# A 4-byte GpSimd mark tile made 128 bytes wide, in an encoder layer on one Trainium2 core: every later on-chip buffer starts 96 bytes higher

## The chip, the cores and the metric

The kernel runs on one NeuronCore of one Trainium2 chip. The metric is the device time of one execution, in microseconds, as the median of several executions. Before the change it is 2389.97 us, the median of 3 (2389.43 to 2391.98). The execution that was profiled took 2390.31 us, and the span from its first to its last instruction is 2388.5 us.

## What is computed

One encoder layer is applied to two inputs of 1024 rows by 1024 channels with the same weights. Cut to what matters:

```python
xn = rmsnorm(x, g_pre)
fv, fg, hv, hg, mg = split(xn @ w_in)                     # 8192 columns
fz  = fftn(fv as (L, 4 groups, 256), axes=(L, 256)).real   # Fourier branch
y_f = (fz * silu(fg)) @ w_fourier_out
v, x1, x2 = split(short_conv(hv, w_short))                # width 3
z = v
for n, gate in enumerate((x1, x2)):                       # Hyena branch
    z = gate * long_conv(z, filters[n], hyena_d[n])       # by FFT of 2L
y_h = (z * silu(hg)) @ w_hyena_out
g_f, g_h = split(sigmoid(mg + b_merge))
out = (g_f * y_f + g_h * y_h) @ w_out
return x + rmsnorm(out, g_post)
```

All data is float32. The filters are made inside the kernel, too.

## The kernel before, in words

A product of two float32 matrices is made of three TensorE products: both factors are split into a rounded high part and a low rest (`split`: ScalarE rounds, VectorE or GpSimd subtracts), and high by high, high by low and low by high are added in PSUM (`mm3`, `times`, and `mm`, whose line 193 issues nearly every product). Every product first loads its stationary factor (128 by 128 floats, 512 bytes in each partition) and then streams its moving factor past it: 512 columns (2048 bytes in each partition) in the large products, 256 to 260 in the transforms.

Four stages follow each other. In the profiled execution they lie about so: the Fourier branch of both inputs (`phase_fourier`, 0 to 200 us); the filters' spectra, with the input projections of the first input between them (`phase_main`, 200 to 680 us); the Hyena branch of both inputs (`branches`, 680 to 1690 us); the remaining gates, the output nets and the last projection (`phase_tail`, from 1690 us).

- `inproj` (from line 838) makes one block of 128 channels of the input projection. Its stationary factors are `wh` and `wl`, in pool `wp`; its moving factors are the 16 tiles `x0..` and `x1..` in pool `xp`, which hold the normalized input. Its sums are called `pin`.
- `forward` and `conv_back` make the transforms of the convolutions: `pX` (tables `cfwd` against `bh`, `bl`) and `pT` (`yh`, `yl` against tables `cinv`), 256 columns each.
- In `phase_tail` the gates (sums `pg`) take some stationary factors from `wp` (`wh`, `wl`, `w`) and some from pool `gw` (`s1h` to `s4l`, `a2h`, `a2l`, `wa`), against moving tiles in `xp` (`x..`, `oB..`) or pool `gs` (`room..`). The nets (sums `pn`) take all of them from `gw` and `xp`, under the names `wh` and `wl` as well.

The change touches `branches` (lines 1100 to 1103). There, `self.due` is a list of 30 transfers that build sums of the output weights in DRAM. They are issued by GpSimd, one in each step of the Hyena branch while the list lasts. Each is held back until a GpSimd copy of one column of the step's result `z` into the tile `mark` has been made, so that it isn't issued earlier. `mark` is the last tile that is asked for from pool `wp`.

Buffers are placed by pool, in the order in which pools are opened, each tile at a multiple of 32 bytes in every partition. `wp` is opened first after the Fourier stage (`open_x`), then `xp`, then the pools of `phase_main` and, in their place, those of `phase_tail`. So the size of `wp` sets where all of these begin. The tiles of the Fourier stage lie in the same space earlier, from pools of their own that begin where `wp` does.

Of the kernel before, what the change touches and what calls it, by code (L numbers as in the profile page):

```python
# [10 lines left out]
F32R = mybir.dt.float32r  # L11
# [5 lines left out]
P = 128  # L17
# [143 lines left out]
class K:  # L161
# [878 lines left out]
    def branches(self, nb, nct, ws):  # L1040

        tc, nc = self.tc, self.nc
        steps = []
        for b in range(nb):
            steps.append((b, 0, 0))
            for c in range(1, nct):
                steps += [(b, 0, c), (b, 1, c - 1)]
            steps.append((b, 1, nct - 1))  # L1050
        plain = list(self.PLAIN)
        Z, X, G = {}, {}, {}

        def front(i):
            b, n, c = steps[i]
            src = self.conv(1, c, ws, "v", b) if n == 0 else Z.pop(c)
            return self.conv_front(src, ws)

        def gates(i):
            b, n, c = steps[i]  # L1060
            x = self.conv(2 + n, c, ws, f"x{n + 1}", b)
            if n and b == 0:
                early = c < NH
                ps = None if early else self.inproj(4, c)
                sg = [self.wp.tile([P, 512], F32, tag="gt", name="sg", bufs=3) for q in range(2)]
                for q in range(2):
                    s = slice(512 * q, 512 * q + 512)
                    if early:
                        nc.sync.dma_start(sg[q], self.d_g[0][4][c][:, s])
                    else:  # L1070
                        nc.scalar.activation(sg[q], ps[:, s], AF.Silu)
                G[i] = sg, early
            X[i] = x

        def close(i):

            if i in G:
                sg, early = G.pop(i)
                for q in range(2):
                    s = slice(512 * q, 512 * q + 512)  # L1080
                    if early:
                        with tc.issue_after(self.rounded.ins):
                            nc.scalar.activation(sg[q], sg[q], AF.Silu)
                    self.mul("dve", X[i][:, s], X[i][:, s], sg[q])
        B = front(0)
        gates(0)
        for i, (b, n, c) in enumerate(steps):
            nxt = None
            if i + 1 < len(steps):
                nxt = front(i + 1)  # L1090
                gates(i + 1)
                if i + 2 < len(steps) and steps[i + 2][0] != steps[i + 1][0]:
                    self.load_x(steps[i + 2][0])
            y = self.conv_back(n, c, B, ws)
            close(i + 1)
            B = nxt
            for _ in range({4: 1, 3: 1, 2: 2, 1: 2}.get(len(steps) - i, 0)):
                self.spill_gate(b, *plain.pop(), ws)
            z = self.gate(n, c, y, X.pop(i))
            if self.due:  # L1100
                mark = self.wp.tile([P, 1], F32R, tag="mark", name="mark", bufs=1)
                with tc.issue_after(nc.gpsimd.tensor_copy(mark, z[:, 0:1]).ins):  # L1102
                    self.due.pop(0)()
            if n == 0:
                Z[c] = z
                continue
            nc.sync.dma_start(self.d_sh[b][c], z)
            if b == 0 and NF <= c:
                self.spill_gate(0, 0, c, ws)
        with tc.issue_after(self.ended.ins):  # L1110
            for sec, c in plain:
                self.spill_gate(1, sec, c, ws)
# [601 lines left out]
```

## Time and profile before

| What | Before |
|---|---|
| median of 3 executions | 2389.97 us |
| profiled execution, its span | 2390.31 us, 2388.5 us |
| TensorE busy | 2341.1 us, 98% of the span, 12784 products |
| VectorE busy | 1971.1 us, 83% |
| ScalarE busy | 1110.1 us, 46% |
| GpSimd busy | 452.9 us, 19% |
| DMA, mean rate | 201 GB/s |
| TensorE clock granted | 0.996 of full speed |

How to read it: products are pipelined. The duration of one in the profile runs from its start to the end of its results, while the next one starts long before. What a product costs a saturated TensorE is the distance from its start to the next one's start, which a stretch of the chain of waits or of the timeline gives when it is divided by the number of products in it. A row of the profile that groups instructions names the line, the engine, the operation, what is written and what is read (moving factor first, stationary factor second), the shapes and the count.

### The profile page before, as it was taken

To read this page: it belongs to the slowest core of one execution; us is meant where nothing else is said; L and a number is where in the kernel's file an instruction comes from. 1 tells how busy PE (TensorE), PEld (TensorE's weight loads), DVE (VectorE), ACT (ScalarE), POOL (GpSimd) and SP (SyncE) were. 2 spreads that over 40 slices of the span, in tenths; PEclk is the share of its full clock that TensorE was granted. 3 is DMA by queue.
4 is the path that set the end of the run, shared out by engine and by line. 5 is a ranking of instruction groups with operands and counts; after the bars stand their busy time and mean duration, and the time that the engine had idled before them with its cause. 6 is when DMAs were issued, how large, how long until landed. Compare 5 with 4: busy or idle time off the path is not lost.

```text
span 2388.5 us, 36189 instructions
## 1 busy us (share of the span) xinstructions
PE 2341.1 (98%) x12784; PEld 2013.8 (84%) x12784; DVE 1971.1 (83%) x3430; ACT 1110.1 (46%) x2072; POOL 452.9 (19%) x428
## 2 busy tenths in 40 slices
PE   6999999999989999999999999999999999999998
PEld 5998888888878888888888888888888888888787
DVE  7775789888788999999888999997655578787987
ACT  6654557767653433334223232333443464556443
POOL 3342231222323333232000000112000000101311
PEclk9999999999999999999999999999999999999999
DMA  7636895555556567667464565455554678998654
GB/s 260 213 135 216 291 322 177 166 170 166 191 184 209 188 213 208 209 196 251 153 201 143 172 189 162 147 159 166 201 164 138 222 257 271 269 311 247 195 160 141
DMA packets 246208, 479.71 MB, mean 201 GB/s; under 512 B 24582, under 2 KB 82280, under 8 KB 245706
## 3 DMA queue, kind: packets, MB, share of 16 engines
q1 hardware_dynamic: 222013, 402.25, 51.8%
q0 software_dynamic: 23792, 75.11, 11.1%
q8 instruction: 101, 1.65, 0.3%
q14 instruction: 81, 0.66, 0.1%
q10 hardware_dynamic: 221, 0.04, 0.0%
HBM read 326.82 MB, written 177.73 MB: 211 GB/s over the span
## 4 chain that ended last, share of the span: by engine, by line
PE 49%; issue 5%; DVE 4%; DMA 3%; POOL 0%; ACT 0%; DVEq 0%; SPq 0%; POOLq 0%; ACTq 0%
PE pin L193 19%; PE pg L193 14%; PE pn L193 5%; PE pT L193 5%; PE pX L193 5%; DMA d_m<-gt 1%; PE tph L904 1%; DVE x L176 0%; DMA oB<-d_wo 0%; DMA g<-d_g 0%; DMA k<-d_k 0%; DVE wl L180 0%; DVE t L180 0%; POOL d_m L1359 0%; DVE gt L180 0%
## 5 line engine op out<-in xcount | busy, mean ns | idle before, releaser
L193 PE MATMUL pin<-x,wh 128*128 128x512 f32 x2816 | 901.9, 396 | 7.5 <-DVE x L176 7.5
L193 PEld LDWEIGHTS pin<-x,wh 128*128 128x128 f32 x2816 | 523.5, 188 | 119.7 <-issue 7.6
L193 PE MATMUL pin<-x,wl 128*128 128x512 f32 x1408 | 558.1, 397 | 0.0
L180 POOL TENSOR_TENSOR wl<-wr,wh 128x512 fp32r<-128x512 f32 x128 | 229.8, 1796 | 670.6 <-ACT wh L170 621.1
L193 PEld LDWEIGHTS pin<-x,wl 128*128 128x128 f32 x1408 | 265.0, 188 | 55.1
L193 PE MATMUL pn<-room,wh 128*128 128x512 f32 x864 | 266.5, 389 | 0.2 <-DVE room L180 0.2
L193 PEld LDWEIGHTS pn<-room,wh 128*128 128x128 f32 x864 | 162.1, 188 | 34.3 <-DVE room L180 0.6
L193 PE MATMUL pn<-room,wl 128*128 128x512 f32 x432 | 168.4, 390 | 0.6 <-DVE wl L180 0.5
L180 DVE TENSOR_TENSOR t<-pX,k 128x1024 f32<-128x1024 f32 x128 | 155.4, 1214 | 10.1 <-PE pX L193 6.8
L193 PE MATMUL pX<-bh,cfwd 128*128 128x256 f32 x768 | 162.2, 288 | 0.0
L193 PE MATMUL pT<-cinv,yh 128*128 128x256 f32 x768 | 145.6, 284 | 1.4 <-DVE T0s L180 1.4
L170 ACT CAST wh<-wr 128x512 fp32r<-128x512 f32 x128 | 79.1, 618 | 142.6 <-PE pin L193 106.2
L170 ACT CAST bh<-b 128x512 fp32r<-128x512 f32 x144 | 88.4, 620 | 113.2 <-DVE b L180 78.8
L193 PEld LDWEIGHTS pT<-cinv,yh 128*128 128x128 f32 x768 | 122.9, 190 | 8.6 <-ACT T1s L957 1.5
L193 PEld LDWEIGHTS pX<-bh,cfwd 128*128 128x128 f32 x768 | 127.1, 190 | 2.6
L1359 POOL DMA_DIRECT2D d_m<-gt x32 | 27.2, 849 | 536.4 <-DVE gt L180 498.1
L170 ACT CAST yh<-y 128x512 fp32r<-128x512 f32 x96 | 59.6, 621 | 126.9 <-DVE y L180 126.4
L180 DVE TENSOR_TENSOR bl<-b,bh 128x512 fp32r<-128x512 f32 x144 | 107.1, 748 | 7.8 <-ACT bh L170 7.7
L193 PE MATMUL pT<-cinv,yl 128*128 128x256 f32 x384 | 109.0, 284 | 0.0
L193 PE MATMUL pX<-bl,cfwd 128*128 128x256 f32 x384 | 109.0, 284 | 0.0
L1102 POOL CAST mark<-x 128x1 fp32r<-128x1 f32 x30 | 21.6, 720 | 411.2 <-DVE x L176 411.0
L180 DVE TENSOR_TENSOR y<-t 128x512 f32<-128x512 f32 x128 | 91.7, 717 | 7.3 <-PE pT L193 6.9
(359 smaller groups left out, 5154.4 us busy)
## 6 DMA issues: line engine op xcount, KB each, us to landing
k<-d_k SPq DMA_DIRECT2D x128, 512.0 KB, 4.2
wr<-in_w_in SPq DMA_DIRECT2D x128, 256.0 KB, 3.4
d_g<-gt SPq DMA_DIRECT2D x124, 256.0 KB, 2.8
wl<-d_s SPq DMA_DIRECT2D x56, 512.0 KB, 5.5
d_k<-kt SPq DMA_DIRECT2D x128, 128.0 KB, 2.3
d_k<-kt SPq DMA_DIRECT2D x64, 256.0 KB, 2.8
g<-d_g SPq DMA_DIRECT2D x64, 256.0 KB, 5.2
r<-d_g SPq DMA_DIRECT2D x60, 256.0 KB, 5.8
```

The costliest lines, as they stand in the source:

```text
L170: self.rounded = nc.scalar.copy(h, src)
L180: return e.tensor_tensor(out, a, b, op=op)
L193: return self.nc.tensor.matmul(out, lhsT, rhs, start=start, stop=stop, skip_group_check=shared)
L904: nc.tensor.transpose(tp[:, q * P:(q + 1) * P], eo[:, e, q], self.ident)
L1102: with tc.issue_after(nc.gpsimd.tensor_copy(mark, z[:, 0:1]).ins):
L1359: nc.gpsimd.dma_start(dst, t, accum_op=ADD)
```

## The change

```diff
             z = self.gate(n, c, y, X.pop(i))
             if self.due:
-                mark = self.wp.tile([P, 1], F32R, tag="mark", name="mark", bufs=1)
-                with tc.issue_after(nc.gpsimd.tensor_copy(mark, z[:, 0:1]).ins):
+                mark = self.wp.tile([P, 32], F32R, tag="mark", name="mark", bufs=1)
+                with tc.issue_after(nc.gpsimd.tensor_copy(mark[:, 0:1], z[:, 0:1]).ins):
                     self.due.pop(0)()
```

The copy still writes one column. On all five engines the same instructions stand in the same order with the same waits as before; only addresses differ. The 4 bytes took a place of 32, and the 128 bytes take a place of 128, so everything behind the tile starts 96 bytes higher. This is where the built programs put some of the tiles (byte in each partition, and what is left when it is divided by 128 and by 512):

```
tile                            before              after
                                byte   /128 /512    byte   /128 /512
wp: wh, first of 3 buffers      17760   96  352     17760   96  352
wp: wr, w, first of 2           30048   96  352     30048   96  352
wp: mark                        40288   96  352     40288   96  352
xp: x00, moving of inproj       40320    0  384     40416   96  480
xp: x10                         44416    0  384     44512   96  480
cfwd / bh                  107904/184192 0  384  108000/184288  96 480
gs: room0                      105856    0  384    105952   96  480
gw: s2h                        181632    0  384    181728   96  480
gw: s4h                        193920    0  384    194016   96  480
nets' wh, in xp                 73088    0  384     73184   96  480
```

Further tiles of a kind follow at multiples of 2048 or 4096 bytes, and the four stationary blocks within a tile at multiples of 512. So before, in the products `pin`, the stationary factor starts 32 bytes short of where the moving factor does, counted modulo 512, and after it 128 bytes short; so it is with those of the `pg` whose stationary factor is in `wp`. In the other `pg` and in `pn`, `pX` and `pT` both factors start at the same place modulo 512, before and after. Tiles that begin before `mark`, and the whole Fourier stage, keep their addresses.

## The prediction

> **What bounds the kernel now.** I read the busy shares first, then the chain of waits, then the groups of products.
>
> ```profile
> PE 2341.1 (98%) x12784; PEld 2013.8 (84%) x12784; DVE 1971.1 (83%) x3430; ACT 1110.1 (46%) x2072; POOL 452.9 (19%) x428
> ...
> L193 PE MATMUL pin<-x,wh 128*128 128x512 f32 x2816 | 901.9, 396 | 7.5 <-DVE x L176 7.5
> ...
> L193 PE MATMUL pin<-x,wl 128*128 128x512 f32 x1408 | 558.1, 397 | 0.0
> ...
> L193 PE MATMUL pn<-room,wh 128*128 128x512 f32 x864 | 266.5, 389 | 0.2 <-DVE room L180 0.2
> ...
> L193 PE MATMUL pn<-room,wl 128*128 128x512 f32 x432 | 168.4, 390 | 0.6 <-DVE wl L180 0.5
> ```
>
> TensorE is busy for 98% of the span, and the largest groups of products wait 7.5 us in all before them. The time is the number of products times the distance between their starts. The reader should look at the mean durations here: products of one shape, 128x512, take 396 or 397 ns as `pin` and 389 or 390 ns as `pn`. The chain of waits, which gives stretches with nothing but products, has the same difference in the distances:
>
> ```profile
> 1659.04 27.76 PE pin L193 x119
> ...
> 1933.88 114.10 PE pn L193 x502
> ```
>
> 27.76 us / 119 = 233.3 ns for a `pin`, 114.10 us / 502 = 227.3 ns for a `pn`. Is it the stage or the operands? The groups of `pg`, which all lie in one stage, answer that (minimum, median and maximum duration, then first and last start):
>
> ```profile
> L193 PE MATMUL pg<-x,wh x176: 393/395/397, 1700.3 to 1897.4; 128*128 128x512 f32 x176
> L193 PE MATMUL pg<-room,s2h x160: 387/389/398, 1692.1 to 2368.5; 128*128 128x512 f32 x160
> ...
> L193 PE MATMUL pg<-oB,wh x120: 393/395/397, 2226.1 to 2360.4; 128*128 128x512 f32 x120
> L193 PE MATMUL pg<-x,s4h x96: 389/389/389, 1705.8 to 1919.2; 128*128 128x512 f32 x96
> L193 PE MATMUL pg<-x,wl x88: 389/394/397, 1700.7 to 1897.6; 128*128 128x512 f32 x88
> ...
> L193 PE MATMUL pg<-oB,s4h x64: 389/389/389, 2243.9 to 2379.4; 128*128 128x512 f32 x64
> L193 PE MATMUL pg<-oB,wl x60: 389/394/499, 2227.4 to 2360.6; 128*128 128x512 f32 x60
> ...
> L193 PE MATMUL pg<-x,wa x24: 389/389/389, 1686.6 to 1691.9; 128*128 128x512 f32 x24
> L193 PE MATMUL pg<-oB,w x12: 393/395/397, 2223.3 to 2225.9; 128*128 128x512 f32 x12
> ```
>
> The same moving tiles `x` and `oB` give 389 ns against `s4h` or `wa` and 394 or 395 ns against `wh`, `wl` or `w`. So it hangs on the stationary factor, and the longer products are exactly those with one from pool `wp`, whose tiles start at 96 modulo 128 bytes where all others start at 0. The timeline of TensorE gives the price: starts 2.10 us apart, then 2.04 us apart, with nine products between them in each case.
>
> ```profile
> 1700.25 0.63 PE L193 MATMUL pg<-x,wh 128*128 128x512 f32 x2
> ...
> 1702.35 0.63 PE L193 MATMUL pg<-x,wh 128*128 128x512 f32 x2
> ```
>
> ```profile
> 1705.84 0.61 PE L193 MATMUL pg<-x,s4h 128*128 128x512 f32 x2
> ...
> 1707.88 0.61 PE L193 MATMUL pg<-x,s4h 128*128 128x512 f32 x2
> ```
>
> 2.10 / 9 = 233.3 ns and 2.04 / 9 = 226.7 ns: a step of 6.6 ns in a product.
>
> **The change part by part.** No instruction is added, removed or moved. The copy into the mark writes the same 128x1, lies on GpSimd and costs what it did. What changes is where the buffers behind it start: 96 bytes higher, although the words of the change say a multiple of 128, since 4 bytes already took 32.
>
> The engines beside TensorE and the transfers first. Before the change some of their operands lie at 96 modulo 128 and others at 0, so the nearest rows bound what the shift costs them:
>
> ```profile
> L170 ACT CAST bh<-b 128x512 fp32r<-128x512 f32 x144 | 88.4, 620 | 113.2 <-DVE b L180 78.8 <-PE pX L193 24.6 <-PE pXf L193 9.0
> ...
> L170 ACT CAST wh<-wr 128x512 fp32r<-128x512 f32 x128 | 79.1, 618 | 142.6 <-PE pin L193 106.2 <-issue 25.1 <-DMA wr<-in_w_in 7.0
> ...
> L180 DVE TENSOR_TENSOR yc<-q 128x512 f32<-128x512 f32 x64 | 41.7, 691 | 0.0
> ...
> L180 DVE TENSOR_TENSOR gt<-gt,g 128x512 f32<-128x512 f32 x48 | 33.2, 691 | 2.0
> ```
>
> ```profile
> wh<-d_w SPq DMA_DIRECT2D x48, 256.0 KB, 3.2
> ...
> x<-d_x SPq DMA_DIRECT2D x32, 256.0 KB, 5.7
> ```
>
> `wh`, `wr` and `gt` lie at 96, `bh`, `b`, `yc` and `q` at 0: ScalarE 618 against 620 ns, VectorE 691 against 691 ns. A load of 256 KB lands after 3.2 us at 96 and after 5.7 us at 0 (in bursts, so this shows only that 96 is not the slow place). I take nothing for all of these, between a gain of 2 ns and a loss of 2 ns in each of the 3430 and 2072 instructions of VectorE and ScalarE, which TensorE covers but for the stretch below.
>
> Now TensorE. Products that take 233.3 ns now: 2816 + 1408 `pin` and, in `pg`, 176 + 88 + 120 + 60 + 12 = 456, in all 4680. After the change their moving factor lies at 96 modulo 128, like their stationary factor, which stays. In the 226.7 ns products both factors lie at 0, and after the change both lie at 96. If what counts is that both start alike modulo 128, then the 4680 come down to the lower distance and the others keep it. I price that with the smaller step, from the chain, 233.3 - 227.3 = 6.0 ns: 4680 x 6.0 ns = 28.1 us. By the timeline's step it is 4680 x 6.6 ns = 30.9 us.
>
> Does all of it reach the end? What is late next is VectorE, where it has no idle time left (busy time and count of PE, PEld, DVE, ACT and POOL in stretches of 100 us; below it PE's for `pin` alone):
>
> ```profile
> 800.00:900.00 100.00, 100.00 (x590) 87.72 (x589) 98.06 (x155) 36.16 (x66) 41.90 (x44) 1.00 0.67 206
> 900.00:1000.00 100.00, 98.65 (x595) 86.95 (x594) 96.44 (x150) 33.41 (x60) 29.43 (x36) 1.00 0.68 210
> 1000.00:1100.00 100.00, 100.00 (x592) 87.72 (x591) 100.00 (x163) 37.46 (x70) 36.88 (x36) 1.00 0.68 196
> 1100.00:1200.00 100.00, 100.00 (x562) 86.36 (x561) 90.27 (x147) 33.64 (x61) 4.24 (x7) 1.00 0.61 207
> ```
>
> ```profile
> 1000.00:1100.00 100.00, 66.94 (x268) 48.08 (x266) 12.70 (x10) 6.65 (x7) 1.00 0.68 196
> ```
>
> In the stretch from 1000 us VectorE is busy for 100.00 of 100 us, so the 268 x 6.0 ns = 1.6 us that TensorE would save there are lost. The two stretches before it have 1.9 and 3.6 us of VectorE left, which is just enough; if VectorE can't use them, three times 1.6 = 4.8 us are lost. The sum: 2390.3 (the profiled execution) - 28.1 + 1.6 = 2363.8 us, so **2364 us**. The median of the runs, 2389.97, lies 0.3 us below the profiled one, which I leave out.
>
> The Trainium skill says the contrary of the premise: the page "TensorE: Matmul & The Clock Gate", in Part 2 under "Step-by-step: what each phase is for", gives TensorE two independent read ports, so that loading the next weights takes no read bandwidth from the running product. Its page "SBUF — State Buffer" counts in lines of 16 bytes (its section on the DMA port swizzle, in the note on cachelines). By these two 96 bytes are six whole lines, nothing meets, and the sum is 2390. The rows above don't agree with that: 395 against 389 ns for the same moving tile.
>
> **The rivals.**
>
> *It stays as it is.* What counts could be a longer period than 128. Modulo 512 the pairs of the 4680 start 32 bytes apart now and 128 bytes apart after the change; only equal starts are seen with 226.7 ns. For this speaks a pair of transforms with 256 columns. In the Fourier stage the factors `eh` and `wo` start 128 apart modulo 512, those of `pT` start alike:
>
> ```profile
> 150.06 0.28 PE L193 MATMUL pfv<-wo,el 128*128 128x256 f32 x1
> ...
> 151.48 0.28 PE L193 MATMUL pfv<-wo,el 128*128 128x256 f32 x1
> ```
>
> ```profile
> 1630.15 0.28 PE L193 MATMUL pT<-cinv,yl 128*128 128x256 f32 x1
> ...
> 1630.87 0.28 PE L193 MATMUL pT<-cinv,yl 128*128 128x256 f32 x1
> ```
>
> 1.42 us / 12 products = 118.3 ns, 0.72 us / 6 = 120.0 ns. So 128 apart isn't the same state as 0 apart. Against it: that state is 1.7 ns shorter there, not longer, so being in it is not itself a loss. This rival gives 2390 us. The two rules of the Trainium skill above would give the same.
>
> *It gets slower.* What counts could be the stationary factor's own address: a start off a multiple of 128 makes a 512-column product 6.6 ns longer, wherever the moving factor lies. Then `pin` keeps its 233.3 ns, and all products of 512 columns in the tail become slow as well: 864 + 432 `pn`, and of `pg` four factors like `s2h` with 160 + 80 each, `s4h` with 96 + 64 and half as many for its low part, and 24 `wa`: 1296 + 960 + 240 + 24 = 2520. 2520 x 6.6 ns = 16.6 us, which gives 2407 us; the place is the tail from 1686 us on, where TensorE is saturated and nothing hides it. It decides as soon as `s2h` at 96 reads 395 ns. Every long row so far fits this as well as my forecast. Against it: stationary tiles of the Fourier stage lie off multiples of 128, and a loss isn't seen there, though only in products of 256 to 260 columns. If `pn` alone were hit, it would be 1296 x 6.6 = 8.6 us, 2399 us.
>
> **How the numbers follow.** Equal starts modulo 128 (forecast): 0.50; it stays: 0.29; slower: 0.21. I prefer the first to the second because one number, equal or not modulo 128, sorts every row of 512 columns above, and because the only row 128 apart costs nothing; the second has the longer period as its one support. The forecast's own range: at best 6.6 ns and the 1.7 ns of the row above together, 4680 x 8.3 ns = 38.8 us, 2352 us; at worst 28.1 - 4.8 = 23.3 us, 2367 us. The whole range reaches from 2352 over 2390 to 2400, which takes in `pn` alone being hit and leaves out most of the last case. A measurement of this kernel tells about 0.2%, 4.8 us, from no change; faster than that 0.50, within it 0.29, slower 0.21.
>
> **What would show it.** Right: `pin<-x,wh` with a mean of 389 ns in place of 396, `pg<-x,wh` at 389/389 and `pg<-x,s4h` still at 389, and some 176 products of `pin` in 40 us of a pure stretch (226.7 ns each). Staying: `pin` at 396 and `pg<-x,s4h` at 389. Slower: `pg<-x,s4h`, `pg<-room,s2h` and `pn` at 395. The forecast would also fail if `pin` came down and the time didn't, which would show as idle time of PE after VectorE between 700 and 1690 us.

## The result, and the profile after

After the change the kernel takes 2389.03 us (median of 22 executions, 2386.13 to 2393.78), before it 2391.74 us (22 executions beside them, 2387.93 to 2400.85). The ratio is 0.999, with a 95% interval from 0.9984 to 0.9996: 2.7 us less, where the forecast had 26 us less. The profiled execution took 2389.24 us, its span is 2387.0 us.

First the busy shares and the groups of products after the change, the rows that the prediction began with:

```profile
PE 2338.9 (98%) x12784; PEld 2018.3 (85%) x12784; DVE 1971.9 (83%) x3430; ACT 1110.0 (47%) x2072; POOL 454.9 (19%) x428
...
L193 PE MATMUL pin<-x,wh 128*128 128x512 f32 x2816 | 900.8, 396 | 7.5 <-DVE x L176 7.5
...
L193 PE MATMUL pin<-x,wl 128*128 128x512 f32 x1408 | 557.9, 396 | 0.0
...
L193 PE MATMUL pn<-room,wh 128*128 128x512 f32 x864 | 266.2, 389 | 0.0
```

The reader is to see that nothing moved between the groups: `pin` still lasts 396 ns in the mean, `pn` 389. The groups of `pg` after the change (minimum, median, maximum) say the same of the tail:

```profile
L193 PE MATMUL pg<-x,wh x176: 390/394/404, 1699.3 to 1896.5; 128*128 128x512 f32 x176
L193 PE MATMUL pg<-room,s2h x160: 387/389/397, 1691.2 to 2366.9; 128*128 128x512 f32 x160
...
L193 PE MATMUL pg<-x,s4h x96: 389/389/395, 1704.9 to 1918.3; 128*128 128x512 f32 x96
```

A small thing did change: `pg<-x,wh` had 393 to 397 ns and now has 390 to 404, so the products are less alike. The chain of waits after the change (start, length, count) has the distances:

```profile
1658.18 27.66 PE pin L193 x119
1685.85 224.92 PE pg L193 x984
```

27.66 us / 119 = 232.4 ns for `pin`, 0.9 ns less than the 233.3 before; `pg` as a whole keeps its 224.9 us (before, `1686.81 224.80 PE pg L193 x984`). Over 4224 `pin` a gain of 0.9 ns is 3.8 us; measured were 2.7, with an interval from 1.0 to 3.8. Engines beside TensorE did not change: VectorE 1971.9 against 1971.1 us, ScalarE 1110.0 against 1110.1.

This is the rival that the prediction calls "It stays as it is", with 2390 us and a chance of 0.29. Its reason, that only starts which are equal by a period longer than 128 give the short distance, is one of the theories of the experiments, which ask what "starting alike" has to mean.

### The profile page after: what moved, and what is told of

Read it like the earlier page. It is cut to its first block, busy times and chain, and to the rows that moved or that the text cites. A ratio compares the mean times of both kernels' runs of the same rounds, so it can differ in the third digit from the quotient of the medians.

```text
span 2387.0 us, 36189 instructions
## 1 busy us (share of the span) xinstructions
PE 2338.9 (98%) x12784; PEld 2018.3 (85%) x12784; DVE 1971.9 (83%) x3430; ACT 1110.0 (47%) x2072; POOL 454.9 (19%) x428
## 4 chain that ended last, share of the span: by engine, by line
PE 53%; DVE 4%; DMA 2%; issue 2%; ACT 0%; POOL 0%; DVEq 0%; SPq 0%; POOLq 0%; ACTq 0%
PE pin L193 19%; PE pg L193 14%; PE pn L193 10%; PE pT L193 5%; PE pX L193 5%; PE tph L904 1%; DMA d_m<-gt 1%; DVE x L176 0%; DMA room<-d_t 0%; DMA k<-d_k 0%; DVE t L180 0%; DVE b L180 0%; DVE wl L180 0%; DMA r<-d_g 0%; DMA xr<-in_x 0%
## 5 line engine op out<-in xcount | busy, mean ns | idle before, releaser
L193 PE MATMUL pin<-x,wh 128*128 128x512 f32 x2816 | 900.8, 396 | 7.5 <-DVE x L176 7.5
L193 PEld LDWEIGHTS pin<-x,wh 128*128 128x128 f32 x2816 | 526.0, 189 | 115.8 <-issue 7.6
L193 PE MATMUL pin<-x,wl 128*128 128x512 f32 x1408 | 557.9, 396 | 0.0
L193 PEld LDWEIGHTS pin<-x,wl 128*128 128x128 f32 x1408 | 266.0, 189 | 53.1
L193 PE MATMUL pn<-room,wh 128*128 128x512 f32 x864 | 266.2, 389 | 0.0
L193 PEld LDWEIGHTS pn<-room,wh 128*128 128x128 f32 x864 | 162.1, 188 | 33.8 <-DVE gt L180 0.2
L193 PE MATMUL pn<-room,wl 128*128 128x512 f32 x432 | 168.4, 390 | 0.9 <-DVE wl L180 0.8
L193 PE MATMUL pX<-bh,cfwd 128*128 128x256 f32 x768 | 162.3, 288 | 0.0
L193 PE MATMUL pT<-cinv,yh 128*128 128x256 f32 x768 | 145.4, 284 | 2.2 <-DVE T0s L180 2.2
L193 PEld LDWEIGHTS pT<-cinv,yh 128*128 128x128 f32 x768 | 122.7, 190 | 9.4 <-ACT T1s L957 2.4
L193 PEld LDWEIGHTS pX<-bh,cfwd 128*128 128x128 f32 x768 | 127.0, 190 | 2.5
L193 PE MATMUL pT<-cinv,yl 128*128 128x256 f32 x384 | 109.0, 284 | 0.0
L193 PE MATMUL pX<-bl,cfwd 128*128 128x256 f32 x384 | 108.9, 284 | 0.0
```

Source lines behind the costliest of these rows:

```text
L193: return self.nc.tensor.matmul(out, lhsT, rhs, start=start, stop=stop, skip_group_check=shared)
```

## The experiments

The seven kernels of the eight runs (one was run twice) have the same instructions in the same order on each engine as the kernel before; only addresses differ. So one number per kind of product tells nearly everything: how far the start of the stationary factor lies from that of the moving factor, modulo 256 or 512. Three theories were tested. The first: only equal starts, by a period longer than 128, give 226.7 ns, wherever the factors lie. The second: it is the place, pool `wp` or the addresses in it, that is slow. The third: distances are only a symptom, and the time would not follow them, since VectorE or something else sets the end.

### The mark ahead of `wp`: both factors start alike

The mark becomes a constant tile, made before `wp` is opened. All of `wp` then starts 32 bytes higher, as do the pools of the Fourier stage, which begin at the same place, and what lies behind `wp` stays: `wh` at 17792 and `x00` at 40320, both 384 modulo 512.

```diff
+        self.mark = cp.tile([P, 1], F32R, name="mark")
...
-                mark = self.wp.tile([P, 1], F32R, tag="mark", name="mark", bufs=1)
-                with tc.issue_after(nc.gpsimd.tensor_copy(mark, z[:, 0:1]).ins):
+                with tc.issue_after(nc.gpsimd.tensor_copy(self.mark, z[:, 0:1]).ins):
```

> The 4-byte mark is taken from the pool of constants, ahead of wp, so wp moves up by 32 bytes and xp and all behind it lie where they did before the change. The stationary factors in wp and the moving factors then start alike modulo 512. Theory (a 512-column product takes 226.7 ns when both factors start alike modulo 512, and 232 to 233 ns when not): pin<-x,wh comes down from 396 to 389 ns, pg<-x,wh reads 389, and 4680 x 6.0 to 6.6 ns less at most 5 us for VectorE gives 23 to 31 us less, 2361 to 2369 us. Rival (the place: factors in wp, at low addresses, cost more wherever they start): pin stays at 396 and the time at 2389 to 2392 us.

Measured: 2371.60 us (2368.33 to 2376.43, 4 executions) against 2391.69 us, a ratio of 0.9911 [0.9891, 0.993]. The chain of waits and the groups of `pg` of this kernel:

```profile
1645.63 27.00 PE pin L193 x119
1672.63 223.04 PE pg L193 x984
```

```profile
L193 PE MATMUL pg<-x,wh x176: 388/389/390, 1686.1 to 1881.5; 128*128 128x512 f32 x176
...
L193 PE MATMUL pg<-x,s4h x96: 388/389/390, 1691.5 to 1903.2; 128*128 128x512 f32 x96
```

27.00 / 119 = 226.9 ns in place of 233.3, and `pg<-x,wh`, still from pool `wp`, now reads like `pg<-x,s4h`. A shift of 32 bytes has done to these products what the shift of 96 bytes was forecast to do. The pool is not slow. The time is 3 us above the expected 2361 to 2369 us; "Why 20 us and not 28" below returns to that.

### The mark in `xp`: the loss moves to other products

The mark is asked for from `xp` in place of `wp`. `x00` comes to 40288 and meets `wh` (17760), both at 352 modulo 512; but the nets' `wh` and the moving tiles `x` and `oB` of the gates lie in `xp` as well, so these come to 352 while their partners in `gs` and `gw` stay at 384.

```diff
-                mark = self.wp.tile([P, 1], F32R, tag="mark", name="mark", bufs=1)
+                mark = self.xp.tile([P, 1], F32R, tag="mark", name="mark", bufs=1)
```

> The 4-byte mark is taken from xp, behind its 16 tiles: the tiles of xp start 32 bytes lower, alike with wp modulo 512, and everything behind xp stays. Theory: pin and the pg with wh, wl or w come down to 389 ns (4680 x 6.3 = 29 us less); what mixes xp with a pool behind it goes up to 394 or 395 ns: pg<-x,s4h and pg<-oB,s4h with their low parts and pg<-x,wa (264), and pn<-room,wh for the stationary tiles that lie in xp, four of five (about 1075), together 1340 x 6.3 = 8 us more; the sum is 2370 us. Rival (the place): pin stays at 396, pg<-x,s4h at 389, 2389 to 2392 us.

Measured: 2378.77 us (2376.89 to 2381.6, 4 executions) against 2391.69, a ratio of 0.9942 [0.9927, 0.9957]. Chain and groups of this kernel:

```profile
1645.54 27.00 PE pin L193 x119
...
1919.49 141.81 PE pn L193 x610
```

```profile
L193 PE MATMUL pg<-x,wh x176: 388/390/398, 1686.1 to 1882.8; 128*128 128x512 f32 x176
...
L193 PE MATMUL pg<-x,s4h x96: 391/395/397, 1691.6 to 1904.7; 128*128 128x512 f32 x96
```

`pin` is short here too (27.00 / 119 = 226.9 ns), at 352 modulo 512, 96 modulo 128. But `pg<-x,s4h` has become the long row and `pg<-x,wh` the short one, the reverse of before, and a stretch of `pn` takes 141.81 / 610 = 232.5 ns. So no address is slow by itself: a factor at 96 modulo 128 is short with a partner at the same place and long with one 32 bytes away. The gain that is missing against the first kernel, 7.2 us, has its place: 1032 `pn` that are 6.5 ns longer make 6.7 us, and 264 `pg` with `s4h`, `s4l` or `wa` that are 6.2 ns longer make 1.6, together 8.3, which the scatter of the two medians covers. So the loss came as expected (8 us); the expected 2370 us was missed because the gain was smaller, as in the first kernel.

### The tail's pool 32 bytes up: the loss alone

The kernel before, with one unused tile of 32 bytes at the head of pool `gw`. `pin` keeps its pair; the gates' factors `s1h` to `s4l`, and some of the nets', start 32 bytes above their moving tiles.

```diff
+            gw.tile([P, 8], F32, name="pad")
```

> The kernel before, with an unused tile of 32 bytes ahead of pool gw. Theory: pin stays at 396 ns; pg<-room,s2h and its like, pg<-x,s4h, pg<-oB,s4h and pg<-x,wa go from 389 to 394 or 395 ns (1224 products), and one in five of pn<-room,wh as well (about 270): 1490 x 6.3 = 9 us more, 2399 to 2402 us. Rival (the place): nothing moves, 2389 to 2392 us.

Measured: 2398.57 us (2393.91 to 2402.94, 10 executions) against 2391.69, a ratio of 1.0027 [1.0017, 1.0036]: 6.9 us slower for 32 unused bytes. Chain and the group of `s2h`:

```profile
1658.71 27.76 PE pin L193 x119
1686.47 229.52 PE pg L193 x984
1927.04 284.71 PE pn L193 x1248
...
2260.55 112.23 PE pg L193 x480
```

```profile
L193 PE MATMUL pg<-room,s2h x160: 391/396/397, 1691.9 to 2374.9; 128*128 128x512 f32 x160
```

The 984 `pg` take 229.52 / 984 = 233.3 ns each, all of them, and the 480 later ones 233.8. The stretches are 4.7 and 2.1 us longer than before (224.80 us, and `2256.37 110.09 PE pg L193 x480`), together 6.8 us. The nets take 284.71 / 1248 = 228.1 ns in the mean, since 264 of them are long too, 6.4 ns each or 1.7 us in all. Over all 1224 `pg` with a factor in `gw`, most of which lie in the two stretches, 6.5 ns make 8.0 us, so the products should cost 9.7 us. Measured were 6.9, with an interval from 4.1 to 8.6 us (0.0017 to 0.0036 of 2391.69). Some of the difference went into waits: from 1915 to 2255 us TensorE is idle for 0.2 us in this kernel's profile and for 1.4 us in that of the kernel before. With that the sum lies at the upper end of the interval. In the tail, then, most of a longer distance passes to the end, though not all of it.

### The tail's pool 256 bytes up: which period

The same with an unused tile of 256 bytes. To make room, three small tiles of the last stage have one buffer in place of two. `s2h` comes to 128 modulo 512, its partner stays at 384: equal modulo 256, as far apart as can be modulo 512.

```diff
+            gw.tile([P, 64], F32, name="pad")
...
-        m = pool.tile([P, n], F32, tag=f"rm{n}", name="rs_m", bufs=2)
+        m = pool.tile([P, n], F32, tag=f"rm{n}", name="rs_m", bufs=2 - (n == 2))
...
-                s1 = op.tile([P, 2], F32, tag="s2", name="s1", bufs=2)
-                rs = op.tile([P, 2], F32, tag="rs2", name="rs", bufs=2)
+                s1 = op.tile([P, 2], F32, tag="s2", name="s1", bufs=1)
+                rs = op.tile([P, 2], F32, tag="rs2", name="rs", bufs=1)
```

> As the one with 32 bytes, with 256 bytes ahead of gw (and three of the small tiles of the last pool with one buffer in place of two, to make room). Theory with a period of 512 bytes: pg<-room,s2h, pg<-x,s4h and pg<-x,wa at 393 to 395 ns, about 8 to 9 us more, 2398 to 2402 us. Rival (a period of 256 bytes): these stay at 389 ns and the time at 2389 to 2392 us.

Measured: 2391.13 us (2390.11 to 2394.14, 10 executions) against 2391.69, a ratio of 0.9997 [0.9988, 1.0007]. Chain and groups:

```profile
1688.41 224.80 PE pg L193 x984
1935.48 271.69 PE pn L193 x1198
...
2256.81 110.08 PE pg L193 x480
```

```profile
L193 PE MATMUL pg<-room,s2h x160: 388/389/390, 1693.7 to 2369.0; 128*128 128x512 f32 x160
```

Both stretches of `pg` have the length that they had before, to 0.01 us, and `pn` takes 271.69 / 1198 = 226.8 ns. 256 bytes apart is the same state as 0 apart; with the change itself, in which 128 apart is long, the period is 256 bytes, where the rival that turned out right had counted modulo 512.

### The best kernel again, and its transforms 96 bytes apart

The first kernel was run a second time, for a narrower interval:

> The kernel with the 4-byte mark in the pool of constants once more, for a narrower interval: by theory and by its first measurement 0.989 to 0.993 of the time before, about 2371 us; by the rival that its first gain was the chip's, nearer to 1.

Measured: 2372.48 us (2371.3 to 2376.97, 5 executions) against 2391.77, a ratio of 0.9922 [0.991, 0.9935]. With it ran the same kernel with an unused tile of 96 bytes ahead of the working tiles of the transforms, so that `pX` and `pT` have factors 96 bytes apart:

```diff
+            wb.tile([P, 24], F32, name="pad")
```

> The same kernel with an unused tile of 96 bytes ahead of pool wb, so that in pX and pT (256 columns) the two factors start 96 bytes apart modulo 256, as those of the Fourier stage do. Theory A (products of 256 columns are not hurt by unequal starts, and pfv is 0.7 ns shorter than pT): pX and pT change by 0 to -0.7 ns, 2300 x -0.7 = -1.6 us, and the time is that of the kernel without the tile within 2 us. Theory B (the transforms also set how the next pin begins, since the first five pin behind a transform are longer): pin changes as well, by up to 6 us in either direction. Rival (unequal starts cost 6.6 ns there, too): pX and pT at 126 ns and 2300 x 6.6 = 15 us more.

Measured: 2373.98 us (2370.86 to 2379.91, 6 executions), a ratio of 0.993 [0.9914, 0.9946]; the two intervals overlap. The mean distance of the 256-column products, worked out from the trace over neighbours with no wait between them, is 119.9 ns for `pX` and 120.1 for `pT`, against 119.1 and 119.0 in the first kernel. The expected shortening by up to 0.7 ns isn't there; they are about 1 ns longer. Over some 1920 products that stand in such pairs, 0.9 ns would be 1.7 us, within what the runs scatter. So at 96 bytes apart products of 256 columns lose about 1 ns where those of 512 lose 6 or 7. Two things go beside this. The expectation puts the factors of the Fourier stage 96 bytes apart; by the built programs those of `pfv<-wo` are 128 apart, as the prediction has it. And the products `pfv<-we` of that stage, with 260 columns, stand at all differences in steps of 16 bytes: in the kernel before they take 118.1 ns at equal starts and 118.5 to 122.0 ns at the others (groups of 12 to 29), so at this size the loss is some 2 ns in the mean.

### 64 and 96 bytes apart

The kernel before, with the mark and an unused tile in `gw` both 64 bytes, or both 96. What lies behind the mark rises by 32 or 64 bytes, so that the stationary factor of `pin` starts 64 or 96 bytes short of the moving one; those of the gates in `gw` start 64 or 96 bytes above theirs.

```diff
-                mark = self.wp.tile([P, 1], F32R, tag="mark", name="mark", bufs=1)
-                with tc.issue_after(nc.gpsimd.tensor_copy(mark, z[:, 0:1]).ins):
+                mark = self.wp.tile([P, 16], F32R, tag="mark", name="mark", bufs=1)
+                with tc.issue_after(nc.gpsimd.tensor_copy(mark[:, 0:1], z[:, 0:1]).ins):
...
+            gw.tile([P, 16], F32, name="pad")
```

(24 in place of 16 in the second.)

> The kernel before with a mark of 64 bytes and an unused tile of 64 bytes ahead of gw: stationary and moving factors start 64 bytes short of each other modulo 256 in pin, 64 bytes past in pg<-room,s2h and its like. Theory (any unequal start modulo 256 costs about the same): both groups at 232 to 233.3 ns from start to start; about 2400 us. Rival (what counts is half a line of 64 bytes, which 32 and 96 miss and 64 does not): both at 226.7 ns and about 2365 us.

> The same with 96 bytes in both places: 96 short in pin, 96 past in pg<-room,s2h and its like. Theory (any unequal start modulo 256 costs about the same): both groups at 232 to 233.3 ns; about 2400 us. Rival (the cost falls with the distance, as 233.1 ns at 32 and 232.2 ns at 128 hint): about 232.5 ns in both.

Measured, one execution each: 2383.03 us with 64 bytes, 2407.26 us with 96, beside a median of 2391.77 for the kernel before. The chain with 64 bytes, then its groups of `pg`; behind them the chain with 96:

```profile
1647.29 27.24 PE pin L193 x119
1674.54 228.43 PE pg L193 x984
```

```profile
L193 PE MATMUL pg<-x,wh x176: 388/391/394, 1688.4 to 1888.3; 128*128 128x512 f32 x176
L193 PE MATMUL pg<-room,s2h x160: 393/394/398, 1680.0 to 2361.7; 128*128 128x512 f32 x160
```

```profile
1664.45 27.76 PE pin L193 x119
1692.21 230.28 PE pg L193 x984
```

With 64 bytes there is an exception to the expected 232 to 233.3 ns and 2400 us: 64 short costs `pin` only 27.24 / 119 = 228.9 ns, and `pg<-x,wh` reads 391 ns, while 64 above costs `s2h` the full step (394). With 96 bytes both sides are long: `pin` 233.3 ns, and the 984 `pg` 230.28 / 984 = 234.0. By the mean distances of the table below, the 64 bytes give 4224 x 4.0 + 456 x 4.4 = 18.9 us and cost (1224 + 264) x 6.5 = 9.7 us, together 9.2 us less; measured were 8.7 less. The 96 bytes should cost some 12 us (1224 x 7.4 + 264 x 7.0 + 4224 x 0.3), and the one execution was 15.5 us longer. The remainder of 3 us isn't explained; one execution can't tell it from scatter.

All runs together, as mean distances between starts in ns, for products of 512 columns (worked out from the traces: neighbours of one kind, no wait between them):

```
stationary start minus moving start,     pin      pg with      other pg   pn
modulo 256                                        wh, wl, w
  0                                      228.3    226.8        226.7      226.8    (before; first kernel)
  0, by 256 bytes apart                  -        -            226.7      226.7    (256 up)
 +32                                     -        -            233.3      233.2    (32 up)
 +64                                     -        -            233.3      233.1    (64 apart)
 +96                                     -        -            234.2      233.8    (96 apart)
 +128 or -128                            232.2    232.7        -          -        (the change)
 -96                                     233.4    233.5        -          -        (96 apart)
 -64                                     229.1    228.9        -          -        (64 apart)
 -32                                     233.1    233.3        -          233.3    (before; mark in xp)
```

The table sorts a product by its own two factors. The timeline of the kernel before shows that a third is at work at the same time, since the weights of the next product are loaded (PEld) while the moving factor of the present one is streamed:

```profile
1633.32 0.39 PE L193 MATMUL pin<-x,wh 128*128 128x512 f32 x1
1633.32 0.19 PEld L193 LDWEIGHTS pin<-x,wl 128*128 128x128 f32 x1
```

Within one kind all stationary factors start alike modulo 512, so the table can't tell a product's own stationary factor from the next one's. The places where one kind of 512 columns follows another can, in the same traces. In the kernel before, a product whose own pair starts alike, ahead of one whose stationary factor starts 32 bytes short of the first one's moving factor (`pg<-room,s1l` ahead of `pg<-x,wh`, above all), takes 235 ns in all 19 such places. The reverse, a product whose own pair is 32 bytes apart ahead of one whose stationary factor starts like the first one's moving factor (`pg<-x,wl` ahead of `pg<-x,s4h`), takes 226 or 227 ns in 18 of 19. With the mark in `xp` there are 20 places where both products have equal pairs, and only the next stationary factor and the present moving one are 32 bytes apart: 234 to 236 ns in all of them. So it is the stationary factor of the next product that has to start where the moving factor of the present one does; in a run of one kind this is the same as an equal pair. Not every such place is as clean: after the change, and with the tail's pool 32 bytes up, the last product of an unequal run still takes 232 to 236 ns although the next weights start like its moving factor. Something from before seems to last for a while there, as in the next section.

### Why 20 us and not 28

The best kernel saves 20.1 and 19.3 us in its two measurements, where the step of 6.0 ns over 4680 products would be 28.1. The table has the reason: `pin` comes down to 228.3 ns, not to 226.8. The timeline of TensorE in the kernel that was run again shows where the rest sits, in a run of 23 `pin` behind a `pT`:

```profile
1639.79 0.28 PE L193 MATMUL pT<-cinv,yl 128*128 128x256 f32 x1
1639.91 0.40 PE L193 MATMUL pin<-x,wh 128*128 128x512 f32 x1
...
1641.07 0.62 PE L193 MATMUL pin<-x,wh 128*128 128x512 f32 x2
...
1645.15 0.40 PE L193 MATMUL pT<-cinv,yh 128*128 128x256 f32 x2
```

The first five take (1641.07 - 1639.91) / 5 = 232 ns each, the 18 behind them (1645.15 - 1641.07) / 18 = 226.7. Over the runs of `pin` in the first kernel (302, of which 241 are longer than one product and have no wait behind the first), the mean distance by the place in the run is 233.1, 234.5, 229.3, 231.7 and 230.3 ns for the first five, 227.5 for the sixth, and 226.7 in the mean from the ninth on. The excess of the first eight adds up to 27 ns in a run of that length, 6.3 us in all. Between kinds of 512 columns there is no such start, as the chain of the same kernel shows:

```profile
1676.10 223.04 PE pg L193 x984
1899.14 5.44 PE pn L193 x24
1904.58 5.44 PE pg L193 x24
```

5.44 us / 24 = 226.7 ns from the first product on. In the Hyena branch, `pin` comes in short runs between transforms of 256 columns, and each run pays again. By the table the saving is 4224 x (233.1 - 228.3) = 20.3 us for `pin` and 456 x 6.5 = 3.0 us for `pg`, together 23.3. The measured 20.1 and 19.3 us are 3 to 4 us short of that. The prediction looked for a loss to VectorE; these are the windows of the first kernel (busy time and count of PE, PEld, DVE, ACT, POOL):

```profile
900.00:1000.00 100.00, 96.24 (x567) 84.71 (x566) 96.07 (x152) 33.97 (x61) 33.11 (x39) 1.00 0.62 193
1000.00:1100.00 100.00, 100.00 (x607) 89.06 (x606) 99.83 (x160) 36.45 (x69) 34.44 (x33) 1.00 0.68 200
```

TensorE is idle for 3.76 us of the first stretch, in the second measurement of this kernel for 2.78, where before it was idle for 1.35. The trace puts both waits down to VectorE (1.51 us until `yl` and 2.26 us until `T0s` in the first kernel). But the kernel after the change, which hardly gained, is idle for 2.24 us there as well, so up to 0.9 of the 2.4 us come without a gain. Between 200 and 700 us it is alike: idle for 10.4 and 11.7 us in the two runs, for 9.0 before and 10.2 after. Longer waits for VectorE are thus a part of the remainder; how large a part, and how much of it is scatter, isn't shown.

## Why the prediction was wrong, point by point

- **What bounds the kernel.** Right. TensorE sets the end, and a change of the distance between starts passes to the time: 6.9 of 9.7 us in the tail with its pool 32 bytes up, 20 of 23 in the best kernel.
- **"So it hangs on the stationary factor."** Right that it isn't the stage, and half right otherwise. In the kernel before, the moving factors of all these rows start at 384 modulo 512, so only the stationary factor seemed to matter. The runs show that it is neither the pool nor an address by itself, but the difference of two starts, and the places where one kind follows another show that the stationary factor that counts is the next product's. This also ends the rival that it gets slower by the stationary factor's own address: after the change `pn` and `pg<-x,s4h`, with both factors at 96 modulo 128, keep 389 ns, where that rival had 395.
- **"If what counts is that both start alike modulo 128."** This is the step that failed. The period is 256 bytes: 256 apart is like 0 apart, 128 apart is not. The change moved the pairs of `pin` from 32 short to 128 short, from one unequal state to another, worth 0.9 ns and not 6.
- **How the choice between the two was made.** The kernel before has pairs of 512 columns at differences of 0 and of 32 short alone, and every period of 64 or more sorts these two alike. "One number sorts every row" was therefore no evidence for 128; it was as good for 256 and 512. The one row that spoke on 128 was `pfv`, and I noted that it isn't in the state of 0 apart, but then weighed it by its price. Its products have 256 columns. At 512 columns the change itself shows 128 apart to be long (232.2 ns); at 256 columns `pfv<-wo`, also 128 apart, takes 118.6 ns over its 342 pairs in the kernel before and `pT` 119.2. So the row could not show the price, and its 1.7 ns, from one short stretch, are 0.6 in the mean.
- **The price.** The step of 6.0 to 6.6 ns in a product was right for long runs (6.4 ns in the run of 119 `pin`, 6.5 in `pg`). As a sum over all `pin` it was too large by a quarter, since the first products of each run behind the transforms stay long: 4.8 ns in the mean, which the chain's long run of 119 could not show.
- **The loss to VectorE.** Not tested by the change, which gained too little. In the best kernel 3 to 4 us are missing, where the prediction had 1.6 to 4.8, but that they agree is in part luck: in the stretch it named, from 1000 us, TensorE is busy for 100.00 of 100 us; longer waits for VectorE, 1.4 to 2.4 us, lie in the stretch ahead of it.
- **The edits at no cost** (VectorE, ScalarE, transfers). Right: 1971.9 against 1971.1 us and 1110.0 against 1110.1 us busy; the loads `wh<-d_w` and `x<-d_x` land after 3.2 and 5.7 us, as before.
- **The Trainium skill.** Its page "TensorE: Matmul & The Clock Gate" (Part 2, "Step-by-step: what each phase is for") has the weight load and the moving factor on independent read ports. The time after the change agrees with what follows from it, but not for its reason. Taken as the prediction took it, no run here should have differed from another, and the medians of several executions lie between 2371.60 and 2398.57 us in kernels that differ in start addresses alone; the places where one kind follows another show the next weight load making the present product longer, 235 ns in place of 226.7.

## What to carry to other kernels

When a row of long durations is sorted by one property of the operands, list the values that this property takes in the trace before believing a rule of it: two values can't tell a period. In this kernel, moving one small tile out of the pool between two large ones, so that both factors of the 512-column products start at the same place modulo 256 bytes, gave a ratio of 0.9922 [0.991, 0.9935]; padding that is meant to align has to be counted from where both pools really start. A price per instruction that was read from a long run holds for long runs; multiply it by the mean over the runs as they come.

## What the runs showed that was not expected

- In float32 products of 128x512, each with a weight load of its own, the distance between starts is 226.7 ns in long runs when both factors start at the same place modulo 256 bytes, and 232 to 234 ns in six of the seven other differences that were measured. In the seventh, the stationary factor 64 bytes short, it is 229. The stationary factor that counts is that of the next product, which is loaded meanwhile. Why 64 short is nearly free while 64 above isn't, stays open.
- Behind products of 256 columns an equal pair needs five to eight products until it reaches 226.7 ns; behind others of 512 columns it has it at once. What settles there, no trace here shows.
- At 256 columns a difference of 96 bytes costs about 1 ns (119.1 against 119.9 ns, 119.0 against 120.1).
- 32 unused bytes at the head of one pool cost 6.9 us of 2391.69, and another pool raised by 32 bytes gained 20: start addresses alone spread the medians of this kernel over 27 us.
